# A diffusion-transformer layer on one core: other transfer times in the attention plan, norm statistics spread by one-pass products, and the last token tile in column halves

## The chip, the cores and the metric

The kernel runs on one core of a Trainium2 chip, in one launch. The metric is device time in microseconds (us). The engines of the core work side by side, each in its own instruction order, and wait for one another by semaphores: TensorE (PE; PEld is its weight load), VectorE (DVE), ScalarE (ACT), GpSimd (POOL) and SyncE (SP), which here only issues DMA transfers. TensorE multiplies a stationary operand (up to 128 x 128, loaded first) with a moving operand of up to 512 columns and adds into PSUM. GpSimd can't read PSUM, so what it is to work on is copied out first.

## The reference, cut to what matters

One layer over 1024 latent tokens of width 1024, with 256 context tokens, all in float32:

```python
mod = silu(c) @ w_mod + b_mod                    # shift1, scale1, gate1, shift2, scale2, gate2
h = x * (1 + scale1) + shift1
proj = h @ w_in + b_in                           # q, k, v of branches A and B, gate logits
o_a = windowed_attention(rope(q_a), ...)         # 8 heads of 64, 2 kv heads, +-128 tokens and context, sink logit
o_b = global_attention(rope(rms(q_b)), ...)      # 8 heads, 2 kv heads, all 1024 + 256 keys
y = (sigmoid(g_a) * (o_a @ w_branch_a) + sigmoid(g_b) * (o_b @ w_branch_b)) @ w_out
x = layer_norm(alpha * x + gate1 * y)            # first norm
h = x * (1 + scale2) + shift2
u = depthwise_conv3(h @ w_up) + conv_b           # 2 x 2816 columns
y = (silu(u_gate) * u_val) @ w_down
x = layer_norm(alpha * x + gate2 * y)            # second norm
```

`layer_norm` takes mean and variance over the 1024 channels of a token.

## The kernel before, in words

Activations lie with channels on the 128 partitions and tokens along the free axis. To keep float32 precision at the one-pass rate of TensorE, operands are split into a rounded `hi` part (type fp32r) and the remainder `lo`, and each product is a triple of matmuls: hi*hi, hi*lo, lo*hi (`mm3`, L376-379). `split` (L367-374) makes the two parts: a rounding copy, then a subtraction.

**Stages in order.** Modulation, projections and rope (to about 336 us); the attention (to about 738); merge, `w_out` and the first norm; the up projection with the convolution, from tile 3 on in products of block sums (half-size products whose sums give the blocks of the result); the down projection in seven half-size products of this kind (numbered 1, 6, 2, 7, 4, 5 and 3); the second norm and the output.

**The attention plan.** 32 units (branch, 128 query tokens, kv group; units 0 to 15 are branch A, 16 to 31 branch B) of scores, softmax, turns (`tr`, L853: transposes of the probabilities), value products (`av`, L862) and output. `graph` lists all operations with a cost (`COST`: engine, time that the engine is taken, time until the result is there) and a sort key: the unit number plus an offset from `KEY`. `plan` (L86-124) simulates the engines: in turn it takes the operation that can start first among the next `LOOK` of each engine, with a slack per engine (`SLACK`) within which the lower key wins. The result is the order in which all five engines' instructions are written; inside this stage nothing reorders them. So the chip's waits come from the difference between the planned and the real times.

Of each unit's turned tiles some are "pooled" (`POOLED`, per branch the places in the unit's list of key tiles): ScalarE copies the turned tile out of PSUM (`cp`) and GpSimd makes both halves (`ph` L1240, `pl` L1251). The others get `hi` from ScalarE (L1245) and `lo` from VectorE (L1251). The value product of the first tile in the list opens the PSUM accumulation, so all others of the unit come after it.

The softmax sums of a unit are inverted (`nr`), turned on PE (`st`), copied (`rc`), written to DRAM (`dn`, L839) and read back spread over the partitions (`rb`, L843, two transfers on SP). GpSimd multiplies the unit's output with them (`tt`, L1276) and splits it (`oh` L879, `ol` L876). In between, groups of the branch product with `w_a` fill in (`grp`, keys from `FILL`), with the gates loaded by SP (`sg`, L1119), and sums of w_down blocks are made by transfers that add in DRAM (`sd` on SP, L891; `sp` on GpSimd's queue, L892).

```python
        rbd = op("rb", kn, lambda u=u: x.rb(u), [dn], uses=[rb])
        rbd.lat = 6.0 if 17 <= u < 30 else 4.2
```

**The norms.** `ln_steps` (L1515-1563) gives the steps of one part of a norm: `stats` (sums of z and z squared over partitions by products with a column of ones; mean, variance, 1/std; GpSimd takes the power -0.5), `diags` (two diagonal matrices, of 1/std and mean/std), `cast` (ones[128,128] times diagonal matrix: each row of the result holds the statistic of all tokens; ScalarE copies it out), and eight `apply` steps, one per channel block. The first norm has parts of 512, 256 and 256 tokens (a0, a1, a2), the second b0 (512) and b1 (256); its last 256 tokens are done by token. The steps are woven into PE's order: `tick` (L1501-1508) adds the columns / 0.8 of each triple to a clock, and when this reaches the due time at the head of the list `pend`, that step is issued. Due times are `LN1_F`, `LN1_D`, `LN2_D`, `LN2_E`: first step, then the gaps to `diags`, `cast`, first apply and each further one. PE's order is as written from the merge on; the other engines' instructions are ordered by the framework when the program is built.

```python
                nc.tensor.matmul(ps, onesf, bcs[i], start=True, stop=True)
                o = post.tile([P, HALF], F32, tag="mrs", name=f"{a}b{nm}", bufs=2)[:, 0:w]
                nc.scalar.copy(o, ps)
```

**The last 256 tokens.** In product 3 they are computed with tokens on the partitions: for each of two tiles of 128 tokens (t = 0, 1) 11 triples of 512 columns go into `yt`; z of all channel blocks is turned by PE (`tok`, L2077). `finish` (L2103-2119) forms u = y * gain + z, takes `bn_stats` of both channel halves, 1/std on GpSimd, and two passes per channel half, (u - mean) * g and then * rstd + b (L2114, L2118), all on VectorE, second half first; SP writes each half out.

## Time and profile before

| | |
|---|---|
| median of 3 runs | 1524.67 us (1518.45, 1525.97, 1524.67) |
| profiled execution | 1521.91 us |
| its span | 1520.0 us |
| mean granted TensorE clock | 0.997 |
| PE busy | 1504.1 us (99%) |
| PEld / DVE / ACT / POOL busy | 1263.4 / 1152.0 / 799.1 / 784.9 us |
| moved by DMA | 229.84 MB |

The span reaches from the first to the last instruction of the profiled execution; the execution's own time is 1.9 us longer. A matmul's busy time overlaps the next one's: a 512-column matmul of 0.39 us is followed by the next after 0.23 us, so the starts of neighbouring rows, not the durations, tell what one costs. In a row of the trace stand start, duration, engine (a q after it: its sequencer, which issues transfers), line, operation, output<-inputs, shape, a count, and in brackets the idle time ahead of it with what ended that.

### The profile page before, as it was taken

Reading aid. Unit: us, or ns where it says so; the run is one execution under the profiler, and the core shown is the slowest. Engines: PE = TensorE matmul, PEld = TensorE weight load, DVE = VectorE, ACT = ScalarE, POOL = GpSimd, SP = SyncE. Lnnn points to the kernel's source line nnn. Section 1 sums busy time; section 2 is a strip of 40 time slices with the busy share of each in tenths; the row PEclk is TensorE's granted clock in tenths of the full one; section 3 lists DMA queues with packets and bytes.
Section 4 is the critical chain, followed back from the end, with each engine's and each line's share of the span. In section 5 each row is a group of like instructions: output and inputs, shape, how many; then the busy total and the mean of one; then the engine's idle time right before and its main releaser. Section 6 shows DMA issues by size and latency. Waiting matters only on the chain.

```text
span 1520.0 us, 21873 instructions
## 1 busy us (share of the span) xinstructions
PE 1504.1 (99%) x7584; PEld 1263.4 (83%) x7584; DVE 1152.0 (76%) x1735; ACT 799.1 (53%) x1406; POOL 784.9 (52%) x744
## 2 busy tenths in 40 slices
PE   9999999999999999999999999999999999999997
PEld 7888888889987888888888998888888888888886
DVE  7588847639886776787675888988888888656897
ACT  6422223449986776798232574444444444435543
POOL 0375303438995666584623556666677764021063
PEclk9999999999999999999999999999999999999999
DMA  9767663313347554823460323333344446997723
GB/s 377 261 215 256 224 237 108 97 39 92 109 145 154 147 123 103 180 63 104 155 156 32 105 84 111 112 111 111 111 105 107 109 113 183 359 289 213 248 88 111
DMA packets 112432, 229.84 MB, mean 151 GB/s; under 512 B 13537, under 2 KB 27617, under 8 KB 112226
## 3 DMA queue, kind: packets, MB, share of 16 engines
q1 hardware_dynamic: 97312, 199.85, 40.1%
q0 software_dynamic: 10400, 20.19, 8.7%
q10 hardware_dynamic: 4610, 8.42, 1.5%
q8 instruction: 59, 0.97, 0.3%
q14 instruction: 51, 0.42, 0.1%
HBM read 177.23 MB, written 65.87 MB: 160 GB/s over the span
## 4 chain that ended last, share of the span: by engine, by line
PE 91%; DVE 3%; POOL 2%; DMA 1%; issue 1%; ACT 1%; SPq 0%; DVEq 0%; POOLq 0%; ACTq 0%
PE av L862 7%; PE pt L853 6%; PE g L377 4%; PE g L378 4%; PE g L379 4%; PE p L377 4%; PE p L378 4%; PE p L379 4%; PE s L760 3%; PE s L761 3%; PE c L379 2%; PE d L379 2%; PE a L379 2%; PE c L378 2%; PE d L378 2%; PE a L378 2%
## 5 line engine op out<-in xcount | busy, mean ns | idle before, releaser
L1251 DVE TENSOR_TENSOR lo<-pt,hi 128x512 fp32r<-128x512 f32 x188 | 128.1, 688 | 51.2 <-ACT hi L1245 44.6
L1245 ACT CAST hi<-pt 128x512 fp32r<-128x512 f32 x188 | 109.6, 583 | 55.1 <-PE pt L853 37.5
L374 DVE TENSOR_TENSOR ld<-rd,hd 128x1024 fp32r<-128x1024 f32 x77 | 97.8, 1288 | 49.4 <-ACT hd L369 47.2
L369 ACT CAST hd<-rd 128x1024 fp32r<-128x1024 f32 x77 | 79.4, 1050 | 85.6 <-PE p L379 54.9
L862 PE MATMUL av<-hi,VT 128*128 128x512 f32 x236 | 100.3, 432 | 3.5 <-POOL hi L1240 3.5
L377 PE MATMUL p<-hd 128*128 128x512 f32 x264 | 103.3, 391 | 0.0
L378 PE MATMUL p<-ld,hd 128*128 128x512 f32 x264 | 102.8, 389 | 0.0
L379 PE MATMUL p<-hd,ld 128*128 128x512 f32 x264 | 102.8, 389 | 0.0
L377 PE MATMUL g<-hh,whg 128*128 128x512 f32 x256 | 99.9, 390 | 0.0
L378 PE MATMUL g<-hl,whg 128*128 128x512 f32 x256 | 99.7, 389 | 0.0
L379 PE MATMUL g<-hh,wlg 128*128 128x512 f32 x256 | 99.7, 389 | 0.0
L862 PE MATMUL av<-lo,VT 128*128 128x512 f32 x236 | 98.7, 428 | 0.8 <-POOL lo L1251 0.7
L374 POOL TENSOR_TENSOR wlg<-wg,whg 128x512 fp32r<-128x512 f32 x32 | 45.1, 1414 | 102.0 <-ACT whg L369 89.5
L799 DVE TENSOR_SCALAR_CACHE_REDUCE p<-s,cvt,nmc 128x1024 f32<-128x1024 f32 x64 | 85.5, 1337 | 12.5 <-PE s L761 6.8
L808 ACT ACTIVATE p<-p,nm 128x1024 f32<-128x1024 f32 x64 | 74.0, 1156 | 9.7 <-DVE p L799 9.7
L853 PEld LDWEIGHTS pt<-ident,p 128*128 128x128 f32 x512 | 63.6, 140 | 17.7 <-DVE lo L1251 0.6
L853 PE MATMUL pt<-ident,p 128*128 128x128 f32 x512 | 76.7, 272 | 0.2 <-DVE lo L1251 0.2
L760 PE MATMUL s<-KL,q 128*128 128x512 f32 (+2 forms) x186 | 73.8, 397 | 0.0
L369 ACT CAST wS<-s 128x512 fp32r<-128x512 f32 x76 | 45.3, 621 | 50.6 <-POOL s L1581 49.7
L761 PE MATMUL s<-KL,q 128*128 128x512 f32 (+2 forms) x186 | 69.6, 374 | 0.5 <-DMA q<-q 0.5
L369 ACT CAST wA<-ru 128x512 fp32r<-128x512 f32 x57 | 35.5, 623 | 60.4 <-PE d L379 32.1
L1251 POOL TENSOR_TENSOR lo<-ptr,hi 128x512 fp32r<-128x512 f32 x48 | 63.6, 1327 | 4.8 <-PE av L862 2.1
(437 smaller groups left out, 5013.2 us busy)
## 6 DMA issues: line engine op xcount, KB each, us to landing
wml<-in_wmodT_dram SPq DMA_DIRECT2D x48, 512.0 KB
ru<-in_w_up_dram SPq DMA_DIRECT2D x38, 512.0 KB
rd<-td SPq DMA_DIRECT2D x55, 256.0 KB
rd<-sd SPq DMA_DIRECT2D x44, 256.0 KB
rd<-in_w_dn_dram SPq DMA_DIRECT2D x33, 256.0 KB
wm<-in_wmodT_dram SPq DMA_DIRECT2D x16, 512.0 KB
wg<-in_w_g_dram SPq DMA_DIRECT2D x32, 256.0 KB
q<-q SPq DMA_DIRECT2D x64, 128.0 KB
```

What stands on the lines that cost most here:

```text
L369: cast[:] = [nc.scalar.copy(hi, src).ins]
L374: low[:] = [lo_eng.tensor_tensor(out=lo, in0=src, in1=hi.bitcast(F32), op=ALU.subtract).ins]
L377: nc.tensor.matmul(ps, a[0], b[0], start=start, stop=False, skip_group_check=resumed)
L378: nc.tensor.matmul(ps, a[0], b[1], start=False, stop=False, skip_group_check=resumed)
L379: return nc.tensor.matmul(ps, a[1], b[0], start=False, stop=stop, skip_group_check=resumed).ins
L760: nc.tensor.matmul(o, self.q1[:, hs], ks, start=True, stop=False)
L761: nc.tensor.matmul(o, self.q2[:, hs], ks, start=False, stop=stop)
L799: nc.vector.tensor_scalar(out=p if self.br else p[:, self.pad + 1:SINK + 1], in0=self.sv[h], scalar1=self.scale()[:, hs] if self.br else - ...
L853: nc.tensor.transpose(tr[:, h * P:(h + 1) * P], src, ident)
L862: nc.tensor.matmul(self.av, v, self.parts[n][low], start=first, stop=self.left == 0)
L1245: nc.scalar.copy(hi, units[u].parts[n])
L1251: e.tensor_tensor(out=lo, in0=src, in1=hi.bitcast(F32), op=ALU.subtract)
```

## The change

Three things. **The plan:** `dn` of units 15 to 17 counts 5.0 us (before 2.2) and their `rb` 9.0 us (before 4.2, for unit 17 6.0); all keys, `FILL`, `LOOK`, `SLACK` have new values; the pooled tile of branch A is the first instead of the second, those of branch B the second and seventh instead of the fifth and seventh. **The norms:** `diags` becomes `rows`: VectorE splits the statistics into hi and lo, PE turns them (4n columns become 4n rows of 128 tokens, into the PSUM tile of the statistics), VectorE copies the rows to SBUF. `cast` then takes for each statistic and each tile of 128 tokens one fp32r product of the rows with one column of `pick`, broadcast to 128, which has ones at the hi and the lo row wanted. The gaps ahead of `rows` and `cast` are shifted for a1 and b1, and a2's `rows` comes after the sixth instead of the fourth apply of a1; the split of the second up weights (1, 0) and (1, 1) is ordered behind a1's row copy instead of its diagonal. **The last tokens:** statistics are taken per 256 columns, tile 1 is multiplied in two column halves with `gain` after each, and in the last pass of the second channel half ScalarE scales and GpSimd adds: all 512 columns of tile 0, 256 of tile 1.

```diff
-LN1_D = (2500.0, 2000.0, 2000.0, 2500.0), (300.0, 3700.0, 300.0, 500.0), (100.0, 1000.0, 300.0, 500.0)
+LN1_D = (2500.0, 2000.0, 2000.0, 2500.0), (2500.0, 1500.0, 300.0, 500.0), (100.0, 1000.0, 300.0, 500.0)
-LN2_E = 3500.0, 1500.0, 1500.0, 500.0, 400.0
+LN2_E = 3500.0, 2000.0, 1000.0, 500.0, 400.0
-POOLED, FILL, SUMS = ((1,), (4, 6)), (17.064666, 27.38753), ('ot1', 'ot1')
-LOOK, SLACK = 32, (0, 0, 0.097929, 0, 0)
+POOLED, FILL, SUMS = ((0,), (1, 6)), (17.167108, 27.943608), ('ot1', 'ot1')
+LOOK, SLACK = 24, (0, 0.113956, 0, 0.006785, 0.086346)
-KEY = {'qh': -1.367635, 'qt': -1.277741, 'sc': -0.147023, 'scs': (0.014781, 0.255647),
-           'scx': -3.68599, 'tr': 0.856601, 'tru': (0.224123, 0.070723),
-           'av': 1.328216, 'st': 1.574664, 'out': 0.027096, 'exd': 1.460316, 'st1': 1.586181, 'wb': (28.660283, 28.120639),
-           'wg': (32.015771, 34.058838, 32.702782, 34.981162), 'ge': -0.859438, 'gr': 3.887651}
+KEY = {'qh': -1.003884, 'qt': -1.205828, 'sc': -0.128011, 'scs': (0.199825, 0.270357),
+           'scx': -3.162255, 'tr': 0.868828, 'tru': (0.216182, 0.070723),
+           'av': 1.348883, 'st': 1.226586, 'out': 0.915147, 'exd': 1.311718, 'st1': 1.601643, 'wb': (28.059869, 29.093441),
+           'wg': (31.732977, 33.079745, 33.170198, 33.633348), 'ge': -0.229045, 'gr': 4.809013}
...
-        rbd.lat = 6.0 if 17 <= u < 30 else 4.2
+        rbd.lat = 9.0 if 15 <= u < 18 else 6.0 if 18 <= u < 30 else 4.2
+        if 15 <= u < 18:
+            dn.lat = 5.0
...
+    lnp = tc.alloc_tile_pool(name="lnp", bufs=1, side="left", reuse_waits="tile")
+    pick = {n: lnp.tile([P, 2 * n], R32, tag=f"pick{n}", name=f"pick{n}") for n in (2, 4)}
+    for n in (2, 4):
+        nc.vector.tensor_tensor(out=pick[n], in0=ident[:, 0:2 * n], in1=ident[:, 2 * n:4 * n], op=ALU.add)
...
+            sp = lnp.tile([P, 16], R32, tag="sp", name=f"sp{nm}", bufs=2)
+            split(rm[:, 0:2 * n], sp[:, 0:2 * n], sp[:, 2 * n:4 * n], nc.vector, nc.vector)
+            sv.extend((sp, st))
-        def diags():
-            bcs.extend(diag(c[:, 0:n], n, f"{a}{nm}") for a, c in zip("rm", sv[2:]))
-            diag_ins[nm] = last_diag[0]
+        def rows():
+            sp, st = sv
+            turned = st[0:4 * n, P:2 * P].bitcast(R32)
+            nc.tensor.transpose(turned, sp[:, 0:4 * n], identr)
+            row = tm(f"row{nm}", R32, w=P)[0:4 * n]
+            row_ins[nm] = nc.vector.tensor_copy(row, turned).ins
+            sv[:] = [row]
...
-                nc.tensor.matmul(ps, onesf, bcs[i], start=True, stop=True)
+                for t in range(n):
+                    w1 = pick[n][0:4 * n, i * n + t:i * n + t + 1].to_broadcast([4 * n, P])
+                    nc.tensor.matmul(ps[:, t * P:(t + 1) * P], w1, sv[0], start=True, stop=True)
...
-                for n, step in zip((a[1], a[3], a[7]), second):
+                for n, step in zip((a[1], a[5], a[7]), second):
...
-                with tc.issue_after(diag_ins["a1"]):
+                with tc.issue_after(row_ins["a1"]):
...
-                nc.vector.bn_stats(out=bst[:, t, 1], in_=zt[1][t])
+                for n in (2, 3):
+                    nc.vector.bn_stats(out=bst[:, t, n], in_=zt[1][t][:, (n - 2) * 256:(n - 1) * 256])
...
+    def gain(t, y, n):
+        if n == 0:
+            u.append(ht(f"ut{t}", (P, HALF)))
+            ot.append(ht(f"ot{t}", (P, 2, HALF)))
+        c = slice(n * 256, (n + 1) * 256)
+        nc.vector.tensor_tensor(out=u[t][:, c], in0=y[:, c], in1=grow[:, c], op=ALU.mult)
+        nc.vector.tensor_tensor(out=u[t][:, c], in0=u[t][:, c], in1=zt[0][t][:, c], op=ALU.add)
+        nc.vector.bn_stats(out=bst[:, t, n], in_=u[t][:, c])
...
-            nc.vector.scalar_tensor_tensor(out=o, in0=o, scalar=rs, in1=lnr[1][:, a], op0=ALU.mult, op1=ALU.add)
+            b = lnr[1][:, a]
+            n = HALF if not a else 256 * t
+            if a:
+                nc.scalar.activation(o[:, n:], o[:, n:], AF.Identity, scale=rs)
+                nc.gpsimd.tensor_tensor(out=o[:, n:], in0=o[:, n:], in1=b[:, n:], op=ALU.add)
+            if n:
+                nc.vector.scalar_tensor_tensor(out=o[:, 0:n], in0=o[:, 0:n], scalar=rs, in1=b[:, 0:n], op0=ALU.mult,
+                                               op1=ALU.add)
...
-        for k in range(NH):
-            h, l = d3[k]
-            mm3(y, (h[:, 1, q], l[:, 1, q]), (h[:, 0], l[:, 0]), k == 0, k == NH - 1)
-            tick(HALF / 0.8)
...
-        finish(t, y)
+        for c in [slice(0, HALF)] if t == 0 else [slice(0, 256), slice(256, HALF)]:
+            for k in range(NH):
+                h, l = d3[k]
+                mm3(y[:, c], (h[:, 1, q], l[:, 1, q]), (h[:, 0, c], l[:, 0, c]), k == 0, k == NH - 1)
+                tick((c.stop - c.start) / 0.8)
...
+            for n in range(c.start // 256, c.stop // 256):
+                gain(t, y, n)
+        finish(t)
```

30 lines of the change are left out of this document (10 added, 20 removed).

## The prediction

> **What bounds the kernel now.** I read the page's engine sums first, then the list of who waited for whom on PE (TensorE), then a table of busy time by stretches of 40 us, and last the order of instructions around the one wait that the list shows.
>
> ```profile
> span 1520.0 us, 21873 instructions
> ...
> PE 1504.1 (99%) x7584; PEld 1263.4 (83%) x7584; DVE 1152.0 (76%) x1735; ACT 799.1 (53%) x1406; POOL 784.9 (52%) x744
> ...
> PE av L862 <- POOL hi L1240: 3.5, 1, 3.5
> ...
> 400.00:440.00 40.00, 40.00 (x282) 35.80 (x281) 32.14 (x73) 37.45 (x88) 37.63 (x57) 1.00 0.27 67
> 440.00:480.00 40.00, 35.74 (x204) 29.73 (x202) 28.07 (x63) 27.46 (x62) 28.06 (x37) 0.96 0.83 214
> ```
>
> The span is 1520.0 us (the execution 1521.91 us with what lies around it) and PE is busy for 1504.1 us of it. So time can be won in two ways only: less work on PE, or less idle time of PE. The longest of PE's waits is a single one of 3.5 us, behind GpSimd. It lies in the stretch from 440 to 480 us, where PE is busy for 35.74 us and its granted clock (the column behind the engines') falls to 0.96. The neighbouring stretch from 400 to 440 us has no idle PE at all. The other idle time is at the end, where the last tile is finished (shown with the tail).
>
> ```profile
> 451.06 0.26 SPq L839 DMA_DIRECT2D dn<-rb  x1
> ...
> 455.53 1.35 POOL L892 DMA_DIRECT2D sd<-in_w_dn_dram  x1
> ...
> 456.12 1.23 SPq L843 DMA_DIRECT2D rb<-dn  x2
> ...
> 464.61 0.72 POOL L1276 TENSOR_TENSOR ot<-ot,rb 128x256 f32<-128x256 f32 x1 [3.45 <-DMA rb<-dn]
> ...
> 467.68 0.61 POOL L1240 TENSOR_SCALAR hi<-ptr 128x512 fp32r<-128x512 f32 x1
> ...
> 468.34 0.73 PE L862 MATMUL av<-hi,VT 128*128 128x512 f32 x2 [3.54 <-POOL hi L1240]
> ...
> 469.00:470.00 1.00, 0.81 (x6) 0.57 (x5) 0.78 (x1) 0.46 (x1) 1.00 (x2) 0.82 1.18 254
> 470.00:471.00 1.00, 1.00 (x4) 0.71 (x4) 1.00 (x3) 0.13 (x1) 0.92 (x2) 0.50 2.54 1028
> ...
> 472.00:473.00 1.00, 1.00 (x4) 0.81 (x3) 0.50 (x1) 1.00 (x2) 0.00 (x0) 0.50 0.38 72
> 473.00:474.00 1.00, 1.00 (x6) 0.83 (x5) 1.00 (x2) 1.00 (x4) 0.00 (x0) 0.97 1.11 258
> ```
>
> These lines tell the wait. The reciprocal sums of unit 15 leave at 451.06 (`dn<-rb`); SP, which must wait until they have landed, starts to spread them over the partitions at 456.12 (`rb<-dn`), 5.1 us later. GpSimd's `tt`, the product that needs them (L1276), can start only at 464.61, 8.5 us after that. GpSimd runs in order, so the `hi` half of a pooled probability tile (L1240) comes at 467.68, and PE waits for it until 468.34. An accumulating transfer of w_down's sums was issued at 455.53, just ahead of the spread. The planner counts 2.2 us for `dn` and 4.2 us for `rb` of unit 15, so it placed the product as if its input would be there 7 us sooner.
>
> The idle time has a second price: the granted clock is 0.82 at 469 us, 0.50 from 470 to 473, 0.97 at 473. That is 0.18 + 3 x 0.50 + 0.03 = 1.7 us of full-speed work lost, though PE counts as busy in it.
>
> **The plan.** The change gives `dn` 5.0 and `rb` 9.0 us in units 15 to 17, which agrees with the 5.1 and 8.5 us above, and brings new keys, another look-ahead, other slacks and other pooled tiles. I take it that the product of unit 15 moves behind the pooled halves on GpSimd, and that the wait and the slow clock go: 3.5 + 1.7 = 5.2 us, **-5.2 us**. No row shows the new order; it has the same products, so I count PE's work as the same. The bounds: 0 where the wait is only moved, and -6.0 where all idle time of that stretch goes (40 - 35.74 = 4.3, and 1.7). With `dn` counted as 5.0 us, SP gets other loads to issue in the 5.1 us in which it sat waiting; the branch loads (`bT`) and query swaps queued behind it come sooner by that, none later. What is late next on GpSimd is `oh` and `ol` of unit 15, which feed the branch groups; they have the whole following unit as cover.
>
> **The norms.** Five steps spread 1/std and mean/std over the partitions: first norm in three parts (512, 256, 256 tokens), second in two (512, 256; the last 256 go by token).
>
> ```profile
> 1461.61 0.86 PE bcrb L1545 x2
> 1462.46 0.86 PE bcmb L1545 x2
> ...
> 865.80 0.59 PE L1545 MATMUL bcra<-dgra,onesf 128*128 128x256 f32 x2
> 866.23 0.59 PE L1545 MATMUL bcma<-dgma,onesf 128*128 128x256 f32 x2
> ...
> 476.32 0.53 PE L739 MATMUL pt<-identr,qs 128*128 128x128 f32 x4
> 476.69 0.46 PE L862 MATMUL av<-hi,VT 128*128 128x512 f32 x1
> ```
>
> Before, each spread is a true-fp32 product of 128 columns of ones with a diagonal matrix: 0.86 us for 512 columns, so 1.72 us for the two, and 0.43 us for 256 (866.23 - 865.80), so 0.86 us. After, it is one turn of a [128, 4n] tile and 2n products of 128 columns in fp32r. The trace has no such product; nearest are four fp32r turns of 128 x 128, which start PE's next operation after 476.69 - 476.32 = 0.37 us, so 0.09 us each (an upper bound would be the 0.2 us of one diagonal half, 0.43/2). With 0.09 a 512-token part costs 9 x 0.09 = 0.83, a 256-token part 5 x 0.09 = 0.46. Saved: 2 x (1.72 - 0.83) + 3 x (0.86 - 0.46) = **-3.0 us**; with 0.2 each it would be -0.3 us.
>
> The Trainium skill ("FP8 and Floating Point Precision", section TensorE Precision Notes) says that true fp32 takes 4 passes through the array. By that a one-pass product of 128 columns is an estimated 0.86/16 = 0.054 us, the saving 2 x (1.72 - 0.49) + 3 x (0.86 - 0.27) = 4.2 us, and the total 1.2 us lower than below; no run here shows it yet, and I keep the row.
>
> Against this stands a new wait. `diags` put nothing on PE; `rows` puts a turn into PE's fixed order, and everything behind it waits until VectorE has split the statistics. Counting the ticks of L1501-1508 (640 for a triple of 512 columns), the turn stands after 3 triples in part a0 (the carried clock is 620), 4 in a1, 3 in a2 (between the applies of a1), 4 in b0, 3 in b1. The triples that start there in the trace, and the last statistic (`mr`) that it needs:
>
> ```profile
> 821.00 0.39 PE L377 MATMUL y<-mh,hwo 128*128 128x512 f32 x1
> ...
> 820.77 0.16 DVE L1536 TENSOR_TENSOR mra<-mva,rsa 128x4 f32<-128x4 f32 x1 [1.22 <-POOL rsa L1535]
> ...
> 863.75 0.39 PE L377 MATMUL u<-B,hwu 128*128 128x512 f32 x1
> ...
> 863.03 0.16 DVE L1536 TENSOR_TENSOR mra<-mva,rsa 128x2 f32<-128x2 f32 x1 [0.59 <-POOL rsa L1535]
> ...
> 870.33 0.39 PE L377 MATMUL u<-B,hwu 128*128 128x512 f32 x1
> ...
> 871.48 0.69 DVE L1536 TENSOR_TENSOR mra<-mva,rsa 128x2 f32<-128x2 f32 x1 [1.29 <-POOL rsa L1535]
> ...
> 1459.40 0.39 PE L377 MATMUL p<-hd 128*128 128x512 f32 x1
> ...
> 1459.72 0.16 DVE L1536 TENSOR_TENSOR mrb<-mvb,rsb 128x4 f32<-128x4 f32 x1 [1.15 <-POOL rsb L1535]
> ...
> 1500.28 0.38 PE L2077 MATMUL zt<-ident,zz 128*128 128x128 f32 x2
> ...
> 1499.46 0.16 DVE L1536 TENSOR_TENSOR mrb<-mvb,rsb 128x2 f32<-128x2 f32 x1 [0.82 <-POOL rsb L1535]
> ```
>
> The split is two more small VectorE operations, an estimated 0.2 us each from the 0.16 us of `mr` and a little for the hand-over. a0: 820.93 + 0.4 - 821.00 = 0.3 us of waiting. a1: 863.19 + 0.4 - 863.75, 0 to 0.3, say 0.1. a2: 872.17 + 0.4 - 870.33 = 2.2, since its chain runs among VectorE's and GpSimd's applies of a1. b0: 1459.88 + 0.4 - 1459.40 = 0.9. b1: ready at 1500.0, 0.3 before it is due, none. Together **+3.5 us**; bounds 1.0 (VectorE, freed of ten diagonal products, reaches a2's chain first) and 6.0 (each chain a further 0.6 us behind other VectorE work). The moved gaps keep their sums (300 + 3700 = 2500 + 1500; 1500 + 1500 = 2000 + 1000, and a2's turn moves from the fourth to the sixth apply of a1), so the spreads are due after the same triples as before. The copy of the turned rows waits on VectorE for PE; queued behind it are the applies and, by the changed order, the splits of the second up weights, 2 to 3 us ahead of their use. The picks are two small operations before the first norm, and hidden.
>
> Of the clock, the rows of the wait at 464 us show it falling some 5 us after PE stopped. The Trainium skill ("TensorE: Matmul & The Clock Gate", What's actually happening) has it fall after an idle window of about 3.4 us; by both, a2's 2.2 us keep the full clock, and I add nothing.
>
> **The tail.** Here VectorE, not PE, ends last.
>
> ```profile
> 1492.05 0.28 PE L378 MATMUL yl<-ld,hd 128*128 128x256 f32 x1
> 1492.17 0.28 PE L379 MATMUL yl<-hd,ld 128*128 128x256 f32 x1
> ...
> 1510.02 0.39 PE L378 MATMUL yt<-ld,hd 128*128 128x512 f32 x1
> 1510.24 0.39 PE L379 MATMUL yt<-hd,ld 128*128 128x512 f32 x1
> ...
> 1509.04 0.42 DVE L1554 TENSOR_TENSOR zz<-zz,mbb 128x256 f32<-128x256 f32 x1
> ...
> 1511.39 0.68 DVE L2107 TENSOR_TENSOR ut<-yt,grow 128x512 f32<-128x512 f32 x1
> ...
> 1515.23 1.41 DVE L2118 SCALAR_TENSOR_TENSOR ot<-ot,bmv,lnr 128x512 f32<-128x512 f32 x2
> ...
> 1512.09 3.06 ACT L1933 ACTIVATE of<-zz,ln2c 128x256 f32<-128x256 f32 x6 [5.40 <-POOL zz L1554]
> ...
> 1516.01 1.04 SPq L2119 DMA_DIRECT2D out_dram<-ot  x2
> ```
>
> PE ends at 1510.63, 9.4 us before the span does, but VectorE takes up the last tile only at 1511.39, being busy with the applies of b1 (the row at 1509.04 is one), and ends at 1516.64. The halved products cost 66 x 0.12 us for 33 x 0.225 (starts of the 256-column pair, and of the 512-column pair): +0.5 us on PE, which the 0.76 us until VectorE comes covers. After the last half, three operations of 256 columns (0.42) stand where three of 512 (0.68) stood: -0.8 us; one of the two last passes is halved: -0.3. Ahead of it VectorE gets six small operations for three in tile 0 (+0.5) and three for the first half of tile 1 (+1.3), and loses one pass (-0.7): it is free 1.1 us later. Sum **0.0 us**. ScalarE and GpSimd take the other half pass; ScalarE has six outputs from 1512.09 to 1515.15, so if that scaling stands behind them it starts at 1515.15, takes 0.4 us, then GpSimd about 0.8, and the transfer starts at 1516.4 instead of 1516.01; the other half's transfer is queued behind it on SP. Bounds -1.3 (VectorE not held up by tile 0) and +1.0.
>
> **Sum.** -5.2 - 3.0 + 3.5 + 0.0 = -4.7 us: 1521.9 - 4.7 = **1517.2 us**. The median of the three runs is 1524.67, 2.8 above the profiled execution (they reach from 1518.45 to 1525.97); a landing that depends on other transfers may well be longer in some, which would make the gain against the median larger, 0.49%.
>
> **Rivals.** (1) *The change does not do what it says*: the late `rb` is met by another GpSimd operation in front of a pooled half, or the shifted branch loads make it later still. For it: the accumulating transfers stay where they were. Then -5.2 is lost: 1522.4 us. (2) *The turns don't wait*: VectorE has room and a2's chain is placed first, the norms give -3.0 + 1.0, the tail -1.3: 1521.9 - 5.2 - 2.0 - 1.3 = 1513.4. Against it: a2's `mr` row is 0.69 us long, a sign of a crowded VectorE. (3) *Slower*: in branch A the pooled tile is now the first (0 for 1), whose `hi` opens the accumulation, so every value product of the unit waits for GpSimd. GpSimd is busy for 37.63 of 40 us in the row from 400 us, 94%, so it has no slack to catch up. At 1.2 us in each of 14 units it would be +17, with the rest 1534. It decides once GpSimd's half comes later than the planner's lag from turn to value (keys 1.35 - 0.87 = 0.48 of a unit) and by 1.1 us in each (1532.3, 0.5% above the median, is 15 us above the forecast, over 14 units); against it, PE waits nowhere in that row and the planner counts GpSimd's time.
>
> **How the numbers follow.** The forecast 0.55 (own range 1514.5 to 1520), the first rival 0.2, the second 0.15, the third 0.1. About 0.5% (7.6 us) is what can be told from no change, so faster means below 1517.0 and slower above 1532.3. The forecast is split by that bound, 0.27 faster and 0.28 same; the first rival is same, the second faster, the third slower. Faster 0.42, same 0.48, slower 0.10. The range for 8 in 10 runs from the second rival, 1513, to just above the first, 1524.
>
> **What would show it.** Plan right: the wait list of PE has no line of 3 us from GpSimd and the stretch around 440 to 480 us shows clock 1.00. Norms: single-pass products at 0.09 us or less, and a line for the turn waiting on VectorE of about 3.5 us, 2 of it in a2. Tail: from PE's end to the span's end still about 9 us. The prediction is wrong if PE waits for `hi` in branch A, or for another transfer in branch B.

## The result, and the profile after

Seven runs of the changed kernel took 1527.34 to 1529.71 us, median 1529.08; seven of the kernel before, beside them on the same chip, 1518.45 to 1525.97, median 1522.58. The ratio is 1.0045, 95% interval 1.0033 to 1.0057: the change makes the kernel 0.45% slower. The profiled execution took 1529.63 us, its span is 1527.9 us, against 1521.91 and 1520.0 before. So 7.9 us came in between these two executions (some 6.9 by the ratio of all runs), where the forecast had -4.7.

From the page of the changed kernel, its span and the engine sums:

```profile
span 1527.9 us, 21990 instructions
...
PE 1506.3 (99%) x7630; PEld 1266.4 (83%) x7630; DVE 1153.8 (76%) x1749; ACT 799.8 (52%) x1408; POOL 780.8 (51%) x746
```

And from the list of what PE waited for in it (line and tile, the releaser, then total in us, count and the longest):

```profile
PE yt L379 <- DVE ut L2117: 6.2, 2, 5.8
PE sta L1543 <- DVE spa L376: 3.3, 2, 3.0
...
PE stb L1543 <- DVE spb L376: 0.9, 1, 0.9
...
PE av L864 <- POOL hi L1242: 0.2, 1, 0.2
```

PE's busy time is 2.2 us larger than before, so most of the 7.9 us is idle time. The 3.5 us behind GpSimd's `hi` have shrunk to 0.2. In their place stand two waits of PE for VectorE: 5.8 us for `ut` in the last tile, and 3.0 us for `spa`, the split statistics of a2 (the list's 3.3 is a2 and a0 together). Where the time came in is seen from the start of each stage's first product on PE:

| first product on PE of | before | after | change since the row above |
|---|---|---|---|
| `y` (`w_out`, after the attention) | 767.6 | 761.5 | -6.1 |
| `u` (up projection) | 860.9 | 855.0 | +0.2 |
| `a` (its products of block sums) | 930.4 | 929.3 | +4.8 |
| `p` (down projection) | 1292.2 | 1291.1 | 0.0 |
| `yl` (product 3, up to the last 256 tokens) | 1475.4 | 1475.1 | +0.8 |
| `yt` (last 256 tokens) | 1492.4 | 1492.8 | +0.7 |
| end of the span | 1520.0 | 1527.9 | +7.5 |

The plan gave 6.1 us. The stage with a2 (from `u` to `a`) took 4.8 of them back, and the tail brought 7.5 more. I go through the three.

**The plan.** Busy time of the engines in stretches of 40 us (PE, PEld, DVE, ACT, POOL, then the granted clock, DMA share and GB/s), changed kernel:

```profile
440.00:480.00 40.00, 39.55 (x235) 32.79 (x234) 31.85 (x71) 32.41 (x75) 31.78 (x41) 1.00 0.75 195
840.00:880.00 40.00, 36.81 (x224) 31.86 (x223) 32.92 (x75) 24.64 (x47) 17.73 (x19) 0.96 0.35 117
```

From 440 to 480 us PE is busy for 39.55 us, where it was 35.74, and the clock is 1.00, where it was 0.96: stall and slow clock are gone. But now 840 to 880 us has 3.2 us of idle PE and a clock of 0.96. That is a2.

**a2.** Its instructions in order of time (start, duration, engine, line, operation; in brackets the idle time ahead and its releaser):

```profile
864.54 0.40 PE L381 MATMUL u<-B,lwu 128*128 128x512 f32 x1
...
865.85 0.71 POOL L1562 TENSOR_TENSOR z<-z,mba 128x256 f32<-128x256 f32 x1
865.90 0.68 DVE L1535 TENSOR_TENSOR rma<-mva,rma 128x2 f32<-128x2 f32 x1 [1.28 <-POOL rma L1534]
...
866.52 0.97 POOL L1589 TENSOR_TENSOR B<-v,B 128x256 fp32r<-128x256 f32 x1
...
866.84 0.69 DVE L375 CAST spa<-rma 128x4 fp32r<-128x4 f32 x1
...
867.77 0.15 DVE L376 TENSOR_TENSOR spa<-rma,spa 128x4 fp32r<-128x4 f32 x1
...
867.98 0.22 PE L1543 MATMUL sta<-identr,spa 128*8 128x128 f32 x1 [3.04 <-DVE spa L376]
```

Two stretches of 3.41 us there, with the columns as in the table by 40 us:

```profile
865.91:869.32 3.41, 1.34 (x7) 1.13 (x8) 3.41 (x10) 2.52 (x5) 1.98 (x3) 1.00 0.33 110
869.32:872.74 3.42, 3.42 (x10) 2.29 (x9) 1.18 (x4) 2.72 (x6) 3.39 (x4) 0.50 0.31 105
```

PE's last matmul ahead begins at 864.54 and ends at 864.94; the turn is next in PE's order and begins at 867.98. In between VectorE takes `rma` at 865.90, the rounding copy at 866.84 and the subtraction at 867.77: from the end of `rma` (866.58) to the end of the split (867.92) it is 1.34 us. Both slow operations run beside one of GpSimd's and end with it: `rma` at 866.58 and the addition from 865.85 at 866.56, the copy at 867.53 and the one from 866.52 at 867.49. The subtraction, with nothing of GpSimd's beside it, takes 0.15 us. That GpSimd is what holds them is read from these ends and was not tried by itself. Then the granted clock is 0.50 from 869.32 to 872.74, while PE is busy all the time: half of 3.42 us, 1.71 us of work lost.

**The products.** b0's spread in the changed kernel, two groups of four products between two triples:

```profile
1461.37 0.40 PE L381 MATMUL p<-hd,ld 128*128 128x512 f32 x1
1461.69 0.66 PE L1553 MATMUL bcrb<-rowb,pick 16*128 16x128 f32 x4
1462.19 0.60 PE L1553 MATMUL bcmb<-rowb,pick 16*128 16x128 f32 x4
1462.72 0.50 PE L379 MATMUL p<-hd 128*128 128x512 f32 x1
1463.06 0.39 PE L380 MATMUL p<-ld,hd 128*128 128x512 f32 x1
```

Four products start every 0.50 us (1461.69 to 1462.19), 0.125 us each. From the start of the last matmul ahead (1461.37) to that of the second behind (1463.06) it is 1.69 us; without the two usual spacings of 0.23 us the eight cost 1.23 us. The turn adds some 0.14 (its start at 1459.38 and the next matmul but one at 1459.75, less 0.23). Before it was 1.72, so a part of 512 tokens saves 0.35 us.

**The tail.** The end of the first column half, what VectorE does then, and the start and the end of the second half:

```profile
1507.36 0.28 PE L381 MATMUL yt<-hd,ld 128*128 128x256 f32 x1
...
1509.39 1.82 DVE L1560 TENSOR_TENSOR zz<-zz,rbb 128x256 f32<-128x256 f32 x2
1509.52 1.41 POOL L2135 TENSOR_TENSOR ot<-ot,lnr 128x512 f32<-128x512 f32 x1 [0.83 <-ACT ot L2134]
...
1511.47 1.27 DVE L1560 TENSOR_TENSOR zz<-zz,rbb 128x256 f32<-128x256 f32 x2
...
1512.67 0.41 DVE L1562 TENSOR_TENSOR zz<-zz,mbb 128x256 f32<-128x256 f32 x1
...
1513.00 0.41 DVE L2117 TENSOR_TENSOR ut<-yt,grow 128x256 f32<-128x256 f32 x1
...
1513.47 0.58 PE L379 MATMUL yt<-hd 128*128 128x256 f32 x1 [5.83 <-DVE ut L2117]
...
1519.32 0.28 PE L381 MATMUL yt<-hd,ld 128*128 128x256 f32 x1
1519.64 0.42 DVE L2117 TENSOR_TENSOR ut<-yt,grow 128x256 f32<-128x256 f32 x1 [5.31 <-PE yt L381]
```

And three stretches of 3.41 us over it:

```profile
1507.61:1511.02 3.41, 0.03 (x1) 0.00 (x0) 3.30 (x6) 1.81 (x3) 2.49 (x3) 1.00 0.23 77
1511.02:1514.43 3.41, 0.96 (x4) 0.96 (x5) 3.24 (x8) 1.82 (x4) 1.68 (x2) 0.50 0.77 254
1514.43:1517.85 3.42, 3.42 (x18) 3.42 (x17) 0.00 (x0) 0.36 (x1) 0.00 (x0) 0.50 0.31 99
```

PE is done with the first half at 1507.64. It can't begin the second, because both halves lie in one PSUM tile and VectorE has yet to read the first: `ut` comes at 1513.00, queued behind the passes of tile 0 and the applies of b1. PE stands for 5.83 us and then works at half clock until 1517.85; from 1513.47 that is 4.4 us at half, 2.2 us lost. From PE's end (1519.60) to the span's end it is 8.3 us, 1.1 less than the 9.4 before. 5.8 + 2.2 + 0.5 (smaller products) - 1.1 = 7.4 of the 7.5 us.

### The profile page after: what moved, and what is told of

It reads as the page before. It is cut to its first block, busy times and chain, and to the rows that moved or that the text cites. A ratio compares the mean times of both kernels' runs of the same rounds, so it can differ in the third digit from the quotient of the medians.

```text
span 1527.9 us, 21990 instructions
## 1 busy us (share of the span) xinstructions
PE 1506.3 (99%) x7630; PEld 1266.4 (83%) x7630; DVE 1153.8 (76%) x1749; ACT 799.8 (52%) x1408; POOL 780.8 (51%) x746
## 4 chain that ended last, share of the span: by engine, by line
PE 91%; DVE 4%; POOL 1%; issue 1%; DMA 1%; ACT 1%; SPq 0%; DVEq 0%; POOLq 0%; ACTq 0%
PE av L864 7%; PE pt L855 6%; PE g L379 4%; PE g L381 4%; PE g L380 4%; PE p L380 3%; PE p L381 3%; PE p L379 3%; PE s L762 3%; PE s L763 3%; PE d L381 2%; PE c L381 2%; PE a L381 2%; PE c L379 2%; PE a L379 2%; PE d L379 2%
## 5 line engine op out<-in xcount | busy, mean ns | idle before, releaser
L855 PEld LDWEIGHTS pt<-ident,p 128*128 128x128 f32 x512 | 63.5, 140 | 17.6 <-ACT rb L837 0.4
```

What stands on the lines that cost most here:

```text
L855: nc.tensor.transpose(tr[:, h * P:(h + 1) * P], src, ident)
```

## The experiments

### Each part alone

**The plan alone** (kernel before, with the new keys, pooled tiles, look-ahead, slacks and both transfer times, nothing of the norms or the tail):

```diff
-POOLED, FILL, SUMS = ((1,), (4, 6)), (17.064666, 27.38753), ('ot1', 'ot1')
-LOOK, SLACK = 32, (0, 0, 0.097929, 0, 0)
+POOLED, FILL, SUMS = ((0,), (1, 6)), (17.167108, 27.943608), ('ot1', 'ot1')
+LOOK, SLACK = 24, (0, 0.113956, 0, 0.006785, 0.086346)
...
+        rbd.lat = 9.0 if 15 <= u < 18 else 6.0 if 18 <= u < 30 else 4.2
```

> Only the plan of the change (transfer times, keys, pooled tiles). Theory A (the plan works as forecast, the loss is elsewhere): 5 to 6 us faster than before, as the first w_out product starts 6.1 us earlier in the changed kernel's trace (761.5 for 767.6 us); no PE wait of over 1 us behind GpSimd. Rival (the plan gains nothing by itself, the gain is of the run): within 2 us of before.

1516.05 us (1515.06 to 1519.37), ratio to before 0.9963 [0.9950, 0.9975], span 1514.3. `y` starts at 761.8, `yt` at 1486.6, both 5.8 earlier than before. The wait that went is not the same in every execution: 3.5 us before, and 2.9, 2.0 and 4.6 us in the traces of the norms alone, the tail alone and the late turns below, which have the old plan. No wait of PE for GpSimd is longer than 0.3 us; the longest left is one of 1.1 us at the program's start.

**The norms alone** (kernel before, with turned rows and one-pass products, and the shifted gaps):

```diff
-        return [(first, stats), (gap, diags), (gap1, cast)] + [
+        return [(first, stats), (gap, rows), (gap1, cast)] + [
```

> Only the norms of the change. Theory A (PE waits for the split of the statistics, and the wait in part a2 also brings the slow clock): 4 to 6 us slower than before, with a wait of about 3 us in a2 and a granted clock of 0.5 for some 3 us after it. Rival (the prediction's sum, -3.0 + 3.5 us): 0 to 1 us slower.

1527.92 us (1522.95 to 1531.8), ratio 1.0039 [1.0020, 1.0059], span 1526.9. PE waits for `spa` (3.0 in a2) and `spb` (1.0). From `u` to `a` it takes 72.8 us, against 69.5 before and 74.3 in the changed kernel: the same wait, and here the clock stays at 1.00 behind it. What this means is taken up below.

**The tail alone** (kernel before, with statistics by 256 columns, column halves, and the pass on ScalarE and GpSimd):

```diff
+        for c in [slice(0, HALF)] if t == 0 else [slice(0, 256), slice(256, HALF)]:
...
+            for n in range(c.start // 256, c.stop // 256):
+                gain(t, y, n)
+        finish(t)
```

> Only the last tokens' part of the change. Theory A (the second column half waits on PE until VectorE has read the first half out of the same PSUM tile, 5.8 us, and then runs 4 us at half clock): 6 to 9 us slower than before. Rival (the prediction's 0.0, bounds -1.3 and +1.0): within 1.3 us of before.

1530.26 us (1525.95 to 1530.89), ratio 1.0056 [1.0035, 1.0076]; PE waits 5.8 us for `ut`. From the start of `yt` to the span's end it is 35.0 us, as in the changed kernel (35.1), against 27.6 before.

So the plan is a gain, and both others are losses. The three ratios multiplied give 1.0058, which lies by the changed kernel's 1.0045 within their intervals.

### Which edit of the plan does it

```diff
-        rbd.lat = 6.0 if 17 <= u < 30 else 4.2
+        rbd.lat = 9.0 if 15 <= u < 18 else 6.0 if 18 <= u < 30 else 4.2
+        if 15 <= u < 18:
+            dn.lat = 5.0
```

> Only the two transfer times in the plan (dn 5.0 us in units 15 to 17, rb 9.0 us), with the old keys, look-ahead and pooled tiles. Theory A (the wait came from these two times): the wait of 3.5 us behind GpSimd at unit 15 and the slow clock after it are gone, 5 to 7 us faster than before. Rival (the new keys are what took the wait away): 2 us faster or less, with a wait of 2 us or more left.

With this alone, all keys as before, it is 1516.36 us (1515.55 to 1517.46), ratio 0.9951 [0.9936, 0.9965]. `y` starts at 761.0. The largest waits of PE in this kernel's list:

```profile
PE cb L525 <- DVE mhalf L407: 1.1, 1, 1.1
PE av L864 <- POOL lo L1253: 0.5, 1, 0.5
PE s L763 <- DMA q<-q: 0.4, 1, 0.4
```

The wait for `hi` is not among them. On GpSimd the product with the late sums (`ot<-ot,rb`) now stands behind both pooled halves:

```profile
462.58 0.61 POOL L1242 TENSOR_SCALAR hi<-ptr 128x512 fp32r<-128x512 f32 x1 [1.17 <-ACT ptr L1237]
...
464.54 0.62 POOL L1242 TENSOR_SCALAR hi<-ptr 128x512 fp32r<-128x512 f32 x1
465.13 0.74 POOL L1278 TENSOR_TENSOR ot<-ot,rb 128x256 f32<-128x256 f32 x1
```

The two truer transfer times are enough for the whole gain; on top of them new keys, other pooled tiles and look-ahead add nothing that can be measured. Whether these would have brought it without the two times was not run.

### The tail taken apart

**The halves in two PSUM tiles** (the changed kernel, with a tile of its own for each column half):

```diff
-        y = sml(f"yt{t}")
         for c in [slice(0, HALF)] if t == 0 else [slice(0, 256), slice(256, HALF)]:
+            y = sml(f"yt{t}_{c.start}")
```

> The changed kernel with the two column halves of tile 1 in PSUM tiles of their own. Theory A (shared tile): the PE wait of 5.8 us and the slow clock are gone, 5 to 8 us faster than the changed kernel, so 1 us faster to 2 us slower than before. Rival (VectorE is late anyway, and sets the end): the PE wait goes but the end stays within 2 us of the changed kernel, 4 to 7 us slower than before.

1523.66 us (1522.67 to 1524.68), ratio to before 1.0009 [0.9999, 1.0019]. The wait of 5.8 us is gone from PE's list:

```profile
PE yt L379 <- DVE ut L2117: 0.4, 1, 0.4
```

The 0.4 us left are not between the halves. They stand ahead of tile 1's first product, in the changed kernel too (its 6.2 us are 5.8 and this) and in the kernel in one piece. So it is the shared tile that stops PE, and VectorE's lateness only sets for how long: VectorE reaches the first half at 1512.60 here, nearly as late, and PE waits no longer for it. The Trainium skill ("PSUM — Partial Sum Buffer", PSUM bank collisions raise a hardware error) has the rule that would have told: accesses of TensorE and VectorE are to be kept apart by bank and quadrant and not by address, so two column ranges of one bank don't make two buffers. The runs agree, 5.8 us in one tile and no wait between the halves in two; that the cause is the bank and not the tile as the unit of the program's waits, they can't show, since here a tile is a bank.

**Tile 1 in one piece** (the changed kernel):

```diff
-        for c in [slice(0, HALF)] if t == 0 else [slice(0, 256), slice(256, HALF)]:
+        for c in [slice(0, HALF)]:
```

> The changed kernel with tile 1 multiplied in one piece of 512 columns; statistics by 256 columns and the part on ScalarE and GpSimd stay. Theory A (the halves only cost by the shared PSUM tile, and VectorE's load sets the end after that): as with two PSUM tiles, 5 us faster than the changed kernel and within 1.5 us of before. Rival (the halves in two PSUM tiles had brought a gain of their own, hidden by the other edits): 1 us or more slower than the run with two PSUM tiles.

1522.47 us (1521.65 to 1523.63), ratio 0.9999 [0.9989, 1.0009]. Both cures take the loss of the tail away but for a rest: from `yt` to the end it is 29.4 us with two tiles and 29.2 with one piece, 1.8 and 1.6 more than before. Two further kernels, both on top of the plan alone with the old norms, ask which edit that is.

**The halves alone** (two PSUM tiles, statistics by 256, all last passes on VectorE):

```diff
+        for c in [slice(0, HALF)] if t == 0 else [slice(0, 256), slice(256, HALF)]:
+            y = sml(f"yt{t}_{c.start}")
```

> The plan, the old norms, and of the tail the column halves of tile 1 in two PSUM tiles with statistics per 256 columns, but all last passes on VectorE. Against the run of the plan alone (1516.05 us, ratio to before 0.9963). My theory of the tail (more and smaller VectorE operations ahead of the last half cost about what the shorter end saves; +0.5 us on PE hidden): 1515.0 to 1516.5. Rival, from the run with two PSUM tiles (VectorE ended 1.6 to 1.8 us later after the last tile's start): the halves carry this, 1517 to 1518. No wait of PE for the gain operation.

**The pass on ScalarE and GpSimd alone** (tile 1 in one piece, old statistics):

```diff
+            n = HALF if not a else 256 * t
+            if a:
+                nc.scalar.activation(o[:, n:], o[:, n:], AF.Identity, scale=rs)
+                nc.gpsimd.tensor_tensor(out=o[:, n:], in0=o[:, n:], in1=b[:, n:], op=ALU.add)
```

> The plan, the old norms, and of the tail only the pass of the second channel half on ScalarE and GpSimd (512 columns of tile 0, 256 of tile 1), with tile 1 in one piece. Against the run of the plan alone (1516.05 us, ratio 0.9963). Theory (VectorE loses 0.7 us of tile 0 and 0.3 us at the end; the GpSimd pass is beside it): 1515.0 to 1516.0. Rival (the pass over ScalarE and GpSimd ends after VectorE's, or holds VectorE up): 1516.5 to 1518, and the last transfer waits for GpSimd.

| kernel | ratio to before | `yt` start to end of span |
|---|---|---|
| before | | 27.6 us |
| plan alone | 0.9963 [0.9950, 0.9975] | 27.7 |
| plan, halves | 0.9958 [0.9943, 0.9973] | 28.2 |
| plan, pass on ScalarE and GpSimd | 0.9957 [0.9942, 0.9973] | 29.1 |
| changed, one piece | 0.9999 [0.9989, 1.0009] | 29.2 |
| changed, two tiles | 1.0009 [0.9999, 1.0019] | 29.4 |
| changed | 1.0045 [1.0033, 1.0057] | 35.1 |

By whole times neither edit can be told from the plan alone. By the traces the halves add 0.5 us and the pass given to ScalarE and GpSimd 1.4, which was meant to relieve VectorE. In the kernel with the pass alone VectorE takes up tile 1 later, 20.1 us behind the start of `yt` against 19.0 in the plan alone, though one pass of 0.7 us was taken off it. Its last two passes, one of them halved, take 1.61 us beside GpSimd's other addition, against 1.41 for two whole ones. GpSimd's part ends before them, at 1512.53 against 1513.08.

What holds VectorE up shows in the multiplications of b1's applies, 256 columns of two operands in SBUF. In the order of time of the plan alone two of them take 0.75 us, beside three additions of GpSimd:

```profile
1503.35 4.22 POOL L1556 TENSOR_TENSOR zz<-zz,mbb 128x256 f32<-128x256 f32 x3 [2.20 <-DVE zz L1554]
...
1503.52 0.75 DVE L1554 TENSOR_TENSOR zz<-zz,rbb 128x256 f32<-128x256 f32 x2
...
1504.53 0.76 DVE L1554 TENSOR_TENSOR zz<-zz,rbb 128x256 f32<-128x256 f32 x2
```

One such addition took 0.74 us at 1499.45 in this trace, so three in 4.22 us means that GpSimd is the one held up here, while VectorE, which was at work first, keeps its rate. In the changed kernel's tail, shown above, it is the other way round: two multiplications take 1.82 us (at 1509.39) beside GpSimd's addition of 512 columns (1.41 us at 1509.52), and end 0.3 us behind it. The work left VectorE, and VectorE lost 1.1 us beside it. The Trainium skill ("SBUF — State Buffer", Who interferes with whom) describes one port pair that VectorE's operations with two SBUF inputs share with GpSimd's that read SBUF, and by its summary the one that is issued second waits until the first has finished; the rows agree, and no run here tests it by itself.

### The norms with the turn put late

**Late turns** (norms alone; the turns of a0, a1, a2 and b0 one to five triples later; in a1 and b0 the gap behind is shorter by as much, in a0 and a2 the spread comes later too):

```diff
-LN1_D = (2500.0, 2000.0, 2000.0, 2500.0), (2500.0, 1500.0, 300.0, 500.0), (100.0, 1000.0, 300.0, 500.0)
+LN1_D = (3100.0, 1900.0, 2000.0, 2500.0), (3100.0, 900.0, 300.0, 500.0), (2200.0, 1900.0, 300.0, 500.0)
-LN2_D = 4000.0, 2800.0, 2000.0, 1200.0, 1300.0
+LN2_D = 4000.0, 3600.0, 1200.0, 1200.0, 1300.0
...
-                for n, step in zip((a[1], a[5], a[7]), second):
+                for n, step in zip((a[1], a[7]), second):
```

> Only the norms of the change, with the turns later in PE's order: one triple later in a0, a1 and b0, after 8 triples instead of 3 in a2 (its spread after 11 instead of 7). Theory A (the waits of PE for the split are the loss, with the slow clock after a2's): no PE wait over 0.3 us for the split, the loss of 6 us is gone and what the products save (about 1 us) remains: 0 to 2 us faster than before. Rival (the turn and the small products themselves cost more, or the later spread delays the up products): 2 us or more slower than before.

1522.32 us (1518.14 to 1524.58), ratio 0.9994 [0.9982, 1.0006]. No wait for a split is left. So the norms' loss is their waits. But without them no gain shows either: of the products' saving (an estimated 1.3 us, worked out below) a new wait takes 0.7 us, of a2's spread for ScalarE, and the rest is too small to be seen.

**Plan and late turns, old tail** (the edits of the plan alone and of the late turns together):

> The plan of the change and the norms with the later turns; the last tokens as before. Theory A (the parts add up): 7 to 9 us faster than before, 1514 to 1516 us. Rival (the parts interact, since the plan's end moves the first norm against the loads): 5 us faster or less.

1516.23 us (1516.07 to 1516.97), ratio 0.9950 [0.9935, 0.9965], span 1514.4. It beats both kernels of this case, and so do the plan alone and the two transfer times alone; the three can't be told apart.

### When does the clock fall?

The wait for a2's split is 3.0 us in the changed kernel, in the one with two tiles, in the one in one piece and in the norms alone. Behind it the clock was halved in the first three, and not in the fourth. First I made the wait shorter (plan and the norms of the change, old tail, a2's turn one and two triples later):

```diff
-LN1_D = (2500.0, 2000.0, 2000.0, 2500.0), (2500.0, 1500.0, 300.0, 500.0), (100.0, 1000.0, 300.0, 500.0)
+LN1_D = (2500.0, 2000.0, 2000.0, 2500.0), (2500.0, 1500.0, 300.0, 500.0), (700.0, 1000.0, 300.0, 500.0)
```

The second kernel has 1400.0 in the place of 700.0.

> The plan and the norms of the change, the old tail, and a2's turn one triple later (gap 700 for 100). Theory (the split's wait is the turn's due time against VectorE's chain, and a triple of matmuls takes about 0.69 us): the wait of PE for a2's split falls from 3.0 to about 2.3 us. Clock, theory A (what counts is the length of the idle time): somewhere below 3.0 us the clock stays at 1.00; by this run it is seen whether 2.3 is below. Clock, theory B (what counts is where the idle time falls against a fixed beat, not its length alone): the clock may fall at 2.3 us too, and the run with 1.7 us need not be the milder. Rival on the wait (VectorE's chain moves with the turn): it stays at 3.0.

> As the run before, with a2's turn two triples later (gap 1400). Theory: wait of PE for a2's split about 1.7 us, and the clock stays at 1.00 if length decides. Rival (chain moves with the turn): 3.0 us.

One execution each, 1520.79 and 1519.73 us, beside 1522.95 for before. From the list of PE's waits, first of the kernel with the turn one triple later:

```profile
PE sta L1543 <- DVE spa L376: 2.6, 2, 2.4
```

And two triples later:

```profile
PE sta L1543 <- DVE spa L376: 1.9, 2, 1.7
```

2.4 and 1.7 us, as expected: a triple later takes some 0.7 us off the wait. Around a2 the clock stayed at 1.00 in both. That would fit a threshold of length between 2.4 and 3.0 us, if it were not for the norms alone. Then I worked out, in every trace, where each drop of the clock begins (from windows of 1 us: a mean of 0.66 in the window from 869 means that the drop begins at 869.32). Within one trace all drops begin whole multiples of 3.413 us apart, to some 0.02 us; in the changed kernel 869.32, 1511.02 and 1524.68 are 188 and 4 such steps apart. Each lasts one step or two, as long as PE has work. From one execution to the next the grid lies elsewhere. And what comes just before: wherever PE waited, a step of the grid in which it was busy for 1.43 us or less was followed by a halved one, and one at full clock with 1.64 us or more was not (drops behind statistics are told of in the last section). One step that was itself halved, behind the wait for `hi` in the norms alone, had 2.47 us of busy PE and was followed by a second halved one; at half clock 2.47 us are the work of 1.24 us. To test this, three more executions of the kernel whose wait is 2.4 us:

> The kernel with a2's turn one triple later again, unchanged (PE waits 2.4 us; the clock stayed at 1.00 there the last time). All drops of the granted clock so far begin, within one trace, on one grid of 3.41 us, last a whole number of grid steps, and follow a grid step in which PE was busy for 1.43 us or less; steps with 1.67 us or more were followed by none. Theory (grid): where a2's wait falls on the grid is chance, so in about six of ten executions (one step holds over 1.85 of the 2.4 us idle) the clock is halved for one step of 3.41 us, which costs 1.71 us. Rival (length): 2.4 us of idle time is too short, the clock stays at 1.00 around a2 in every execution.

> As the run before it, a further execution of the same kernel. Grid: half clock for one step behind a2's wait in about six of ten, and just where the step of the grid (known from the drop at the end of the program) has PE busy for less than about 1.5 us. Length: never.

> As the two before it. Grid: half clock behind a2's wait just where the step of the grid has PE busy for less than about 1.5 us; over the three the chance that it never comes is about 0.06. Length: never.

1519.82, 1519.83 and 1520.56 us. In the last of them the turn and its wait are

```profile
866.89 0.27 PE L1543 MATMUL sta<-identr,spa 128*8 128x128 f32 x1 [2.37 <-DVE spa L376]
```

and three steps of its grid, as a table of busy time by stretches (PE first; the clock is the third number from the end):

```profile
863.39:866.80 3.41, 1.14 (x5) 0.58 (x4) 2.12 (x7) 2.09 (x6) 3.02 (x4) 1.00 0.57 199
866.80:870.21 3.41, 3.32 (x9) 2.67 (x10) 1.99 (x7) 2.83 (x6) 2.32 (x3) 0.50 0.23 77
870.21:873.63 3.42, 3.42 (x17) 2.62 (x16) 2.58 (x8) 2.45 (x7) 1.46 (x2) 1.00 0.25 81
```

In the execution before it, the same two views:

```profile
867.67 0.22 PE L1543 MATMUL sta<-identr,spa 128*8 128x128 f32 x1 [2.38 <-DVE spa L376]
```

```profile
866.29:869.70 3.41, 2.03 (x10) 1.64 (x10) 3.25 (x10) 3.17 (x6) 1.98 (x2) 1.00 0.35 117
869.70:873.11 3.41, 3.41 (x17) 2.65 (x16) 1.33 (x4) 2.60 (x6) 2.71 (x4) 1.00 0.25 79
```

And the steps of the first of the three:

```profile
865.90:869.31 3.41, 1.66 (x8) 1.40 (x9) 3.41 (x11) 2.84 (x6) 1.98 (x3) 1.00 0.39 129
869.31:872.72 3.41, 3.41 (x18) 2.58 (x17) 1.17 (x4) 2.88 (x7) 3.07 (x4) 1.00 0.24 80
```

The same kernel with the same wait of 2.4 us: where one step of the grid takes nearly all of it and PE is busy there for 1.14 us, the next step runs at 0.50; where it is spread so that PE keeps 2.03 or 1.66 us, the clock stays. Length alone falls by this. In four executions of this kernel it came once, where I expected six in ten; three is too few to say whether that share is wrong.

The Trainium skill ("TensorE: Matmul & The Clock Gate", What's actually happening) states that the clock is set by an activity window of 3413 ns which runs free of the kernel. The traces agree with this to 0.02 us. Its table lets the clock fall after an idle window; here windows in which PE was busy for up to 1.43 of 3.41 us were enough.

## Why the prediction was wrong

- **What bounds the kernel:** right. Nearly all of the change in time is idle or slowed PE, and VectorE at the end.
- **The plan, -5.2 us:** right in mechanism and size: 5.8 us earlier at `y` with the plan alone, 5.6 us by its ratio (0.37% of 1522). With the two times alone the product does move behind the pooled halves; in the changed kernel its spread is also issued earlier (452.26 for 456.12), and it comes at 462.82, between two of them, without a wait. That the size fits so well is in part luck, since the wait was 2.0 to 4.6 us in the traces with the old plan. The 1.7 us of slow clock was one grid step. The first rival (the wait is only moved) fell, and so did the third (branch A's first tile pooled): PE's longest wait for `hi` is 0.2 us.
- **The norms' products, -3.0 us:** the step that fell is "so 0.09 us each". They take 0.125 us apart, and 1.23 for the eight with what stands around them. A 512-token part saves 0.35 us instead of 0.89; for the five parts together I get an estimate of 1.3 us (two at 0.35, and three of half the size at 0.2 each). The row that I took, a turn of four blocks, was no measure of products whose stationary operand is one column broadcast. The bound beside it was added up wrongly too: with 0.2 us each the forecast's sum is a loss of 0.6 us (2 x 0.08 + 3 x 0.14), not -0.3. The Trainium skill's four passes ("FP8 and Floating Point Precision", TensorE Precision Notes), by which I had 4.2 us, would have led further off.
- **The norms' waits, +3.5 us:** 0.2 (a0), 0.15 (a1), 3.0 (a2), 0.95 (b0), 0 (b1), together 4.3. Four of five were right to 0.2 us. In a2 the failed term is "two more small VectorE operations, an estimated 0.2 us each": in the crowd of a1's applies the split took 1.34 us and not 0.4, the copy alone 0.69, as `mr` had there. I took `mr`'s 0.69 us for a sign of a crowded VectorE; it too ended with an addition of GpSimd's (`mr` at 872.17, the addition from 871.42 at 872.16).
- **The clock, "a2's 2.2 us keep the full clock, and I add nothing":** failed. 1.71 us were lost in the changed kernel. I took the delay of the fall in one trace for a length that a wait must have; it is a grid step with little work in it, and 2.4 us can bring it.
- **The tail, 0.0 us:** this is the step that decided. "+0.5 us on PE, which the 0.76 us until VectorE comes covers" takes for granted that PE runs through both halves. In the code the two halves write column ranges of one tile, `y[:, c]`, with `gain` reading it between them; the wait of 5.8 us stands in it, and with the clock it made +8.0, more than the whole +7.5. I had even counted VectorE as 1.1 us later at that point. My term for the shorter end, -1.1 us, seems met behind PE's end (9.4 to 8.3), but by luck: 0.7 of it is that VectorE, which PE had kept waiting, was there at once. From its multiplication with the gain to the span's end it was 8.6 us before (from 1511.39) and 8.3 now (from 1519.64). The sign that I named, some 9 us from PE's end to the span's end, was met while the sum failed, since it does not tell when PE ends.
- **The pass given away:** I counted it as 1.0 us off VectorE (0.7 in tile 0, 0.3 at the end). By the traces it adds 1.4 us to the tail.
- **The rival on the slower side** had its place in the attention, where GpSimd is 94% busy. The place was the two new points at which PE's fixed order passes a result of VectorE's.

Sum: -6.1 (plan) + 6.5 (from `y` to `yt`) + 7.5 (tail) = +7.9 us. Of the 6.5, waits, clock and products explain 4.3 + 1.7 - 1.3 = 4.7; of the other 1.8 us, 0.6 stands in the stage of `yl` in the plan alone too (17.6 us against 17.0), and 1.2 us stays open. An estimated 0.7 of that is four times the 0.17 us by which a matmul's 0.40 us exceed the spacing of 0.23, which each wait costs besides.

## What to carry to other kernels

When a product is cut into pieces so that another engine can begin earlier, ask for each piece whether it has a buffer of its own: with one PSUM tile for both, PE's second half waits for the reader of the first, and the reader's whole queue stands ahead of it. A step that puts another engine's result into PE's fixed order costs what that engine's queue holds at that moment, so it is to be placed by the rows of the small operations in that stretch, and of GpSimd's beside them, not by what they take alone, with some triples to spare. Where a planner is given latencies, measure first the one transfer that is late: here its two times alone brought as much as with new keys on top.

## What the runs showed of the hardware

**The clock's grid.** In each of the 11 traces that have more than one drop of the granted clock, all begin on one grid of 3.413 us, which lies elsewhere in each execution. Where PE waited, a step with at most 1.43 us of busy PE was followed by one at 0.50, which costs 1.71 us; a step at full clock with 1.64 us or more by none. So a wait of 2.4 us sometimes costs 1.7 us more and sometimes nothing, and single executions of one kernel can differ by that much.

**Busy is not activity.** In four traces the clock also fell behind b0's statistics, 16 products with one column each. In each of the four, 14 to 16 of the products and a wait of 0.18 to 0.29 us between them lie in the step ahead of the fall. Busy time by steps of the grid in one of them, the plan with the halves (products from 1448.15 to 1450.3, the wait 0.28 us):

```profile
1447.67:1451.08 3.41, 3.13 (x23) 2.81 (x22) 3.31 (x5) 0.47 (x1) 0.00 (x0) 1.00 0.44 141
1451.08:1454.49 3.41, 3.41 (x10) 2.65 (x9) 2.19 (x7) 1.04 (x1) 1.03 (x1) 0.50 0.80 270
```

PE is listed as busy for 3.13 of 3.41 us, and yet the next step runs at 0.50. In eight other traces all 16 products lie in one step too, with no wait over 0.11 us between them, and the clock stayed at 1.00. So it did in the changed kernel:

```profile
1453.00:1456.41 3.41, 3.41 (x24) 3.10 (x23) 3.37 (x4) 0.23 (x2) 0.00 (x0) 1.00 0.47 138
```

It also stayed in the kernel with two tiles, where 15 of the products and a wait of 0.29 us lie in one step:

```profile
1451.37:1454.78 3.41, 3.12 (x23) 2.75 (x21) 3.31 (x4) 1.44 (x2) 0.61 (x1) 1.00 0.50 156
```

So the busy time that is listed does not decide it: 3.12 us kept the clock and 3.23 us, in the kernel with a2's turn one triple later, did not. Small products seem to count for little there; what tips such a step stays open, since this is read from the traces and was not tried by itself. The fall is 1.7 us of what the spans of the kernels with the halves or the pass (1516.5 and 1516.6 us) lie above that of the plan alone (1514.3).

**VectorE beside GpSimd.** VectorE's pair of multiplications took 1.82 us beside an addition of GpSimd's that began ahead of the second of them, and 0.75 us where VectorE was at work first; there it was GpSimd that needed 4.22 us for three additions. In a2 operations of two and four columns took 0.68 and 0.69 us beside GpSimd's and 0.15 without. An engine that is given work to relieve another can hold it up.
